# The first token group of a hybrid attention and mLSTM block: small inputs in one array, low weight parts on VectorE, a third stage tile

## The chip, the cores and the metric

The kernel runs on one core of one Trainium2 chip. The metric is the time of one execution in device microseconds. The kernel before takes 1304.31 us, the median of three runs (1303.35 to 1304.36).

## What is computed

One layer of an encoder trunk. A conditioning vector c gives a shift, a scale and a gate; x is RMS-normalised, scaled and shifted; one wide projection feeds a neighbourhood-attention head group and a bidirectional mLSTM head group; an output projection, the gated residual and a final RMSNorm follow. The part that matters here is the beginning:

```python
c_act = jax.nn.silu(c)
mod = c_act @ w_ada + b_ada
shift, scale, gate = jnp.split(mod, 3, axis=-1)
h = rmsnorm(x, norm_w) * (1.0 + scale) + shift
proj = h @ w_in + b_in        # 2048 tokens, D = 1024, over 4600 columns
...
x = rmsnorm(x + gate * (mixed @ w_out), final_norm_w)
```

Everything is in float32. The two mixers lie far behind the change.

## The kernel before

The 2048 tokens are worked on in four groups of 512 (g = 0 to 3), D in eight steps of 128 (k = 0 to 7). h is kept transposed, with D on the partitions. A product in float32 is made of three faster ones: h is held as a high part `hhi` and a low part `hlo`, a weight block as `whi` and `wlo`, and each product adds hi x hi, hi x lo and lo x hi. The high part is a copy by ScalarE into the type that rounds, the low part a subtraction of raw and high; until now VectorE makes some of these low parts of the weights and GpSimd (POOL) the others.

The front is the method `start`. It is recorded in the order in which it is written (a manual schedule), so each engine's instructions stand as the code has them. Its parts, in order:

- Loads. ScalarE's queue loads the conditioning vector `cact`, a row of it `c_all`, the shift's and scale's bias `bada` and the norm weight `nw`; SyncE's queue (SP) loads x tile by tile, eighteen tiles `mod_*` of the modulation matrix, pieces of the first two weight blocks (`load_p`), and the sixteen gate columns `rg`. Each SP load takes one of eight semaphores in turn and so waits until the eighth load before it has landed.
- TensorE runs matmuls on constants, `dense`, five of them, then spreads c over the partitions (`c`), then four more.
- The sums of squares of x tiles 0 to 3 (ScalarE and VectorE in turn), their inverse roots, and the scaling of x.
- The modulation: for step 0, and for the shift of step 1, TensorE forms it with matmuls of one column (`column`). For all else VectorE does: `mod(n)` is one dot product of a loaded tile with `c_all`; even n gives the scale `gT`, odd n the shift `shT`, of step n // 2.
- The eight k steps of group 0. `turned(k)` transposes x on TensorE, `first_h(k)` makes `hhi` and `h` on ScalarE and returns the subtraction `low` for VectorE; `split_p` makes the weight parts; `products(k)` issues 24 matmuls into two blocks' banks, `firsts` and `seconds`. A third weight block (`raw_w(2, 2, ...)`) goes to a borrowed tile `w_extra`.
- The evictions of groups (`vo_group`): VectorE adds the bias and writes a stage tile `stvo`, ScalarE applies a sigmoid to half of it, and a store takes it to the scratch `d_ck`. Two stage tiles take turns (`stage_tile`). In group 0 three weight blocks are evicted: 0, 1 and the one in `w_extra`. GpSimd sets a column of each stage to one before it is used.
- h for groups 1 to 3 comes from a transposed copy of x (`load_t`) through `make_h` (VectorE, ScalarE, VectorE), which needs the roots of its group spread by TensorE (`rb`, line 286). `next_h` hands these out between the evictions: for group 1, it begins behind the third tile of the third weight block. `vo_first` then issues the products of the next group, k by k.
- From there on the schedule goes to the table fills `d_t`, the token blocks and all later phases.

Of the kernel before, what the change touches and what calls it, by code (L numbers as in the profile page):

```python
# [8 lines left out]
F32 = mybir.dt.float32  # L9
F32R = mybir.dt.float32r  # L10
AF = mybir.ActivationFunctionType
ALU = mybir.AluOpType
# [3 lines left out]
P = 128  # L16
D = 1024
# [41 lines left out]
class Kernel:  # L59
    def __init__(self, tc, x, x_p, x_t, cT, c_row, w_mod, w_gt, b_ada, norm_w, w_main, w_gate, b_col, b_row, b_gate, conv_w, conv_b,  # L60
                 rpb, ml_w, w_out, fnw, out):
        self.tc, self.nc = tc, tc.nc
        self.x, self.x_p, self.x_t, self.cT, self.c_row, self.w_mod, self.w_gt = x, x_p, x_t, cT, c_row, w_mod, w_gt
        self.b_ada, self.norm_w = b_ada, norm_w
        self.w_main, self.w_gate, self.b_col, self.b_row = w_main, w_gate, b_col, b_row
# [151 lines left out]
    def start(self, left):  # L217
# [4 lines left out]
        badd = ada.tile([P, 2 * KT], F32, name="bada")  # L222
        nw = ada.tile([P, KT], F32, name="nw")
        nwb = ada.tile([P, KT], F32, name="nwb")
        cb = ada.tile([P, D], F32, name="c_all")
        cact = ada.tile([P, KT], F32, name="cact")
# [101 lines left out]
        rg = xp.tile([P, KT, 16], F32, name="rg")  # L328
        nc.sync.dma_start(rg, self.w_gate)
# [13 lines left out]
        for n in range(9):  # L343
            if n == 5:
                for j, ps in enumerate(wide):
                    nc.tensor.matmul(ps, self.ones[0:1, :], cb[0:1, j * GT : (j + 1) * GT], start=True, stop=True)
            nc.tensor.matmul(dense[:, :240], self.ident, self.big, start=True, stop=True)
# [27 lines left out]
        for tt in (1, 3):  # L375
            scale_x(tt, rst, slice(2 * P, D), nc.vector)
# [45 lines left out]
        parts, ssqs = [], {}  # L422
# [6 lines left out]

        for k in range(KT):  # L430
# [41 lines left out]
        ssqs[1] = xp.tile([P, 4], F32, tag="ssq", bufs=2, name="ssq_1")  # L472
# [29 lines left out]
        for g in range(NG):  # L502
# [26 lines left out]
            else:  # L529
# [7 lines left out]
                self.vo_group(2, 2, 0, brow=brow, tops=tops)  # L537
# [11 lines left out]
    def gate_row(self, pool):  # L549
# [3 lines left out]
        nc.sync.dma_start(cact, self.cT)  # L553
# [108 lines left out]
    def vo_group(self, h, slot, g, first=None, brow=None, tops=()):  # L662
        nc = self.nc
        st = self.stage_tile(f"stvo_{h}_{g}")
# [1140 lines left out]
_INS = ['x', 'x_p', 'x_t', 'cT', 'c_row', 'w_mod', 'w_gt', 'b_ada', 'norm_w', 'w_main', 'w_gate', 'b_col', 'b_row', 'b_gate', 'conv_w', 'conv_b', 'rpb', 'ml_w', 'w_out', 'fnw']  # L1805
# [3 lines left out]
def layout(inputs):  # L1809
# [16 lines left out]
    def block(n):  # L1826
# [12 lines left out]
        "cT": a["c"][0].reshape(KT, P).T,  # L1839
# [3 lines left out]
        "b_ada": a["b_ada"][0][: 2 * D].reshape(2 * KT, P).T,  # L1843
        "norm_w": a["norm_w"][0].reshape(KT, P).T,
        "w_main": np.stack([block(n) for n in range(len(blocks))]),
        "w_gate": w3[:, :, GATES:],
# [34 lines left out]
```

## Time and profile before

| | |
|---|---|
| median of three runs | 1304.31 us |
| the profiled execution | 1305.46 us |
| its span, first to last instruction | 1303.7 us |
| mean granted TensorE clock | 0.989 |
| DVE, ACT, POOL busy | 61%, 41%, 20% of the span |
| HBM traffic | 204 GB/s over the span |

The page divides the span into 40 slices; the first three of the TensorE clock read 7, 9 and 8 tenths, the others 9 or more. Those three are the front. A busy TensorE in these pages isn't TensorE at its peak, as matmuls are pipelined; what is read here is when it is idle, and which instruction it waits for. Line numbers are those of the kernel before.

### The profile page before, as it was taken

To read this page: it belongs to the slowest core of one execution; us is meant where nothing else is said; L and a number is where in the kernel's file an instruction comes from. 1 tells how busy PE (TensorE), PEld (TensorE's weight loads), DVE (VectorE), ACT (ScalarE), POOL (GpSimd) and SP (SyncE) were. 2 spreads that over 40 slices of the span, in tenths; PEclk is the share of its full clock that TensorE was granted. 3 is DMA by queue.
4 is the path that set the end of the run, shared out by engine and by line. 5 is a ranking of instruction groups with operands and counts; after the bars stand their busy time and mean duration, and the time that the engine had idled before them with its cause. 6 is when DMAs were issued, how large, how long until landed. Compare 5 with 4: busy or idle time off the path is not lost.

```text
span 1303.7 us, 22944 instructions
## 1 busy us (share of the span) xinstructions
PE 1277.4 (98%) x8170; PEld 1103.3 (85%) x8170; DVE 794.7 (61%) x2384; ACT 532.3 (41%) x1172; POOL 258.6 (20%) x385
## 2 busy tenths in 40 slices
PE   9889999999999999999999999999999999999997
PEld 8889999999888887788888888888877878778776
DVE  5876353112567565166677877777657676767664
ACT  4444243543234222123333323333357555555551
POOL 1400002441000000102212002212224332332541
PEclk7989999999999999999999999999999999999999
DMA  9799955997678763745756767656688744655551
GB/s 365 260 293 295 254 195 136 253 234 193 189 179 197 173 153 97 202 122 161 198 164 201 246 195 220 211 176 169 201 252 276 225 156 154 201 179 171 169 167 66
DMA packets 217514, 259.08 MB, mean 199 GB/s; under 512 B 23867, under 2 KB 164027, under 8 KB 217400
## 3 DMA queue, kind: packets, MB, share of 16 engines
q1 hardware_dynamic: 142294, 186.48, 49.8%
q0 software_dynamic: 13616, 37.28, 9.1%
q10 hardware_dynamic: 61490, 33.85, 9.1%
q8 instruction: 65, 1.06, 0.3%
q14 instruction: 49, 0.40, 0.1%
HBM read 173.05 MB, written 92.72 MB: 204 GB/s over the span
## 4 chain that ended last, share of the span: by engine, by line
PE 77%; issue 5%; ACT 3%; DVE 3%; DMA 2%; POOL 1%; POOLq 0%; SPq 0%; ACTq 0%; DVEq 0%
PE pq L1046 24%; PE y L1611 7%; PE pc L605 4%; PE pc L606 4%; PE pc L604 4%; PE pvo L604 3%; PE pvo L606 3%; PE pvo L605 3%; PE pO L1568 3%; PE pT L1553 2%; PE pv L606 2%; PE pv L605 2%; PE pv L604 2%; PE pS L1522 2%; PE pi L1285 2%
## 5 line engine op out<-in xcount | busy, mean ns | idle before, releaser
L1046 PE MATMUL pq<-hhi,whi_a 128*128 128x512 f32 x512 | 208.3, 407 | 0.9 <-ACT u L951 0.9
L1046 PE MATMUL pq<-hlo,whi_a 128*128 128x512 f32 x512 | 208.3, 407 | 0.0
L1046 PE MATMUL pq<-hhi,wlo_a 128*128 128x512 f32 x512 | 207.1, 405 | 0.9 <-POOL wlo_a L1020 0.9
L1046 PEld LDWEIGHTS pq<-hhi,wlo_a 128*128 128x128 f32 x512 | 96.7, 189 | 17.6 <-POOL wlo_a L1020 1.3
L1046 PEld LDWEIGHTS pq<-hhi,whi_a 128*128 128x128 f32 x512 | 96.7, 189 | 17.4 <-ACT u L951 1.3
L1046 PEld LDWEIGHTS pq<-hlo,whi_a 128*128 128x128 f32 x512 | 96.8, 189 | 16.2 <-issue 0.6
L1020 POOL TENSOR_TENSOR wlo_a<-rawq,whi_a 128x1024 fp32r<-128x1024 f32 x19 | 45.5, 2395 | 295.8 <-ACT whi_a L1019 284.1
L1534 ACT ACTIVATE ring<-ring,mn 128x480 f32<-128x480 f32 (+5 forms) x128 | 76.0, 595 | 56.9 <-DVE mn L1533 56.6
L1555 ACT ACTIVATE ring<-pT 96x384 f32<-96x384 f32 (+3 forms) x128 | 65.6, 513 | 64.1 <-PE pT L1553 62.3
L1611 PE MATMUL y<-hhi,wlo_a 128*128 128x512 f32 (+1 forms) x272 | 89.7, 396 | 0.6 <-ACT y L1618 0.6
L1611 PE MATMUL y<-hhi,whi_a 128*128 128x512 f32 x256 | 88.6, 410 | 0.0
L1288 ACT ACTIVATE num<-px,gtile 128x129 f32<-128x129 f32 x120 | 38.3, 366 | 112.4 <-PE px L1283 83.7
L1460 POOL DMA_DIRECT2D v<-d_vna x158 | 79.0, 506 | 26.0 <-DMA v<-d_vna 6.3
L1307 POOL TENSOR_TENSOR hm<-hm,ck 128x128 f32<-128x128 f32 x64 | 27.5, 430 | 250.1 <-DVE hm L1306 213.8
L1553 PEld LDWEIGHTS pT<-ident,ring 128*128 128x128 f32 (+2 forms) x416 | 50.4, 136 | 26.9 <-ACT ring L1555 12.3
L1553 PE MATMUL pT<-ident,ring 128*128 128x128 f32 (+2 forms) x416 | 67.0, 274 | 3.9 <-ACT ring L1555 3.9
L1533 DVE CUSTOM_DVE_ANT_0 ring<-pS,tab 128x480 f32<-128x480 f32 (+5 forms) x128 | 62.4, 540 | 7.1 <-PE pS L1522 6.0
L604 PE MATMUL pvo<-whi_b,hhi 128*128 128x256 f32 x224 | 64.0, 286 | 0.5 <-DVE gates L678 0.5
L606 PE MATMUL pvo<-whi_b,hlo 128*128 128x256 f32 x224 | 63.2, 282 | 0.0
L605 PE MATMUL pvo<-wlo_b,hhi 128*128 128x256 f32 x224 | 63.2, 282 | 0.0
L893 ACT ACTIVATE dec<-dec,gtile 128x128 f32<-128x128 f32 x128 | 41.4, 391 | 46.9 <-POOL dec L886 36.6
L676 DVE TENSOR_TENSOR stvo<-pvo,brow 128x256 f32<-128x256 f32 x60 | 24.9, 420 | 58.3 <-PE pvo L606 43.4
(336 smaller groups left out, 3371.4 us busy)
## 6 DMA issues: line engine op xcount, KB each, us to landing
ck<-d_ck SPq DMA_DIRECT2D x64, 384.5 KB, 3.5
rawq<-in_w_main_dram SPq DMA_DIRECT2D x28, 512.0 KB, 4.5
raw<-in_w_main_dram SPq DMA_DIRECT2D x18, 512.0 KB, 5.8
kv<-d_ck SPq DMA_DIRECT2D x64, 128.5 KB, 3.2
dec<-d_mneg SPq DMA_DIRECT2D x32, 256.0 KB, 6.1
d_ck<-dec ACTq DMA_DIRECT2D x32, 256.0 KB, 6.6
d_ck<-stvo SPq DMA_DIRECT2D x15, 514.0 KB, 4.5
d_qna<-qst ACTq DMA_DIRECT2D x30, 256.0 KB, 4.5
```

Of the source, the lines that this page charges most:

```text
L604: nc.tensor.matmul(ps, lhi(k), rhi(k), start=(k == 0), stop=False)
L605: nc.tensor.matmul(ps, lhi(k), rlo(k), start=False, stop=False)
L606: self.mark = nc.tensor.matmul(ps, llo(k), rhi(k), start=False, stop=(k == KT - 1))
L893: nc.scalar.activation(t[:, o, :], t[:, o, :], AF.Exp, bias=self.cols["g"][:, d, h, c : c + 1])
L1020: (eng or nc.gpsimd).tensor_tensor(lo[:, :, cs], raw, hi[:, :, cs].bitcast(F32), ALU.subtract)
L1046: self.mark = nc.tensor.matmul(patch_ps(ps) if patch else ps, w, self.htok(h, g, k, patch), start=(k == 0 and n == 0), stop=(k == KT - 1 a ...
L1460: queue.dma_start(chunks[key][r * nkc : (r + 1) * nkc, :], rows[r])
L1533: nc.vector.tensor_tensor_reduce(pt[:, :nk], ps, tabs[ct][:, j * nk : (j + 1) * nk], 1.0, 3e38, ALU.add, ALU.min, mn)
L1534: nc.scalar.activation(pt[:, :nk], pt[:, :nk], AF.Exp, bias=mn, scale=-1.0, accum_out=sums[:, j : j + 1])
L1553: nc.tensor.transpose(ps[:cs, i, :], U[u][j][:, i * cs : (i + 1) * cs], self.ident)
L1555: nc.scalar.activation(t[:cs, :nch, :], ps[:cs, :nch, :], AF.Copy)
L1611: nc.tensor.matmul(y, m[:, k, :], w[k][:, cs], start=(k == 4 and n == 0), stop=(k == 3 and n == 2))
```

## The change

It has five parts.

1. The conditioning vector, the bias, the norm weight and the gate columns are laid out beside each other in one array `small`, 160 numbers to a partition. One load on ScalarE's queue replaces three there and one on SP.
2. TensorE runs 12 `dense` matmuls instead of 9: five before c is spread, as before, and seven behind it instead of four.
3. All low parts of weights in the front are made by VectorE: six pieces of blocks 0 and 1, and the two halves of `w_extra`, which move a little in the order (`high_w2`, `low_w2`). GpSimd has none left.
4. `mod(2)`, the scale of step 1, is summed ahead of the first low part of h; the rest of x's tiles 1 and 3 is scaled behind the second block's first low part. The four sums of squares for group 1 are all made by ScalarE; VectorE made two of them.
5. The third stage of group 0 has a tile of its own, `stvo_third`. The two old stage tiles go on taking turns without it.

The core of the diff:

```diff
-        nc.scalar.dma_start(cact, self.cT)
+        nc.scalar.dma_start(small, self.small)
         nc.scalar.dma_start(cb[0:1, :], self.c_row)
-        nc.scalar.dma_start(badd, self.b_ada)
-        nc.scalar.dma_start(nw, self.norm_w)
...
-        rg = xp.tile([P, KT, 16], F32, name="rg")
-        nc.sync.dma_start(rg, self.w_gate)
...
-        for n in range(9):
+        for n in range(12):
...
-        for tt in (1, 3):
-            scale_x(tt, rst, slice(2 * P, D), nc.vector)
+        mod(2)
...
+        def load_w2(half):
+            w2.append(self.raw.tile([P, 4, 256], F32, tag=f"raw{half}", name=f"raw_2_{half}"))
+            nc.sync.dma_start(w2[half], self.w_main[2, :, 4 * half : 4 * half + 4, :])
+
+        def high_w2(half):
+            nc.scalar.activation(self.wslot[2][0][:, 4 * half : 4 * half + 4, :], w2[half], AF.Copy)
+
+        def low_w2(half):
+            hi, lo = (part[:, 4 * half : 4 * half + 4, :] for part in self.wslot[2])
+            nc.vector.tensor_tensor(lo, w2[half], hi.bitcast(F32), ALU.subtract)
...
+                for tt in (1, 3):
+                    scale_x(tt, rst, slice(2 * P, D), nc.vector)
...
-            if k + 1 < KT:
+            if 0 < k < KT - 1:
                 mod(2 * k + 2)
...
-            if k:
+            if 0 < k < KT - 1:
                 low()
...
-                    split_p(b, (k + 1) // 2)(nc.gpsimd)
+                    split_p(b, (k + 1) // 2)()
             if k in (1, 4):
-                parts += self.raw_w(2, 2, (k // 4,))
+                load_w2(k // 4)
...
-            if k in (5, KT - 1):
-                parts[k // 6]()
+            if k in (KT - 3, KT - 2):
+                high_w2(k - KT + 3)
+            if k == KT - 2:
+                low_w2(0)
+            if k == KT - 1:
+                for tt in range(4, 8):
+                    square(tt, ssqs[1])
+                low()
+                low_w2(1)
...
-        for j in (0, 2):
-            dot(xt[4 + j], xt[4 + j], 1.0, 0.0, ssqs[1][:, j : j + 1])
-            square(5 + j, ssqs[1])
...
-                self.vo_group(2, 2, 0, brow=brow, tops=tops)
+                third = xp.tile([P, 1032], F32, name="stvo_third").rearrange("p (o c) -> p o c", o=4)
+                self.vo_group(2, 2, 0, brow=brow, tops=tops, stage=third)
...
-        st = self.stage_tile(f"stvo_{h}_{g}")
+        st = self.stage_tile(f"stvo_{h}_{g}") if stage is None else stage
```

How it moves the instructions, in the order of each engine. VectorE at the first low part, from the first subtraction for weight block 0 (`wlo_a`) on; ISA rows are dot products (`junkv`) and the reads of their sums. Before:

```order
L364 TENSOR_TENSOR wlo_a<-rg,whi_a 128x8x16
L276 TENSOR_SCALAR x_167<-x_167,rst_223 128x768
L276 TENSOR_SCALAR x_171<-x_171,rst_223 128x768
L390 TENSOR_TENSOR hlo_103<-h_0_280,hhi_102 128x512
L316 TENSOR_TENSOR wlo_b<-wr_0_178,whi_b 128x512
L260 ISA junkv_293,gT<-mod_hi,c_all,nwb,nw 128x1024
L260 ISA gT 128x1
L260 ISA junkv_339,gT<-mod_lo,c_all,nwb,nw 128x1024
```

and of the change:

```order
L359 TENSOR_TENSOR wlo_a<-small,whi_a 128x8x16
L259 ISA junkv_261,gT<-mod_hi,c_all,nwb,small 128x1024
L259 ISA gT 128x1
L384 TENSOR_TENSOR hlo_103<-h_0_278,hhi_102 128x512
L315 TENSOR_TENSOR wlo_b<-wr_0_172,whi_b 128x512
L275 TENSOR_SCALAR x_163<-x_163,rst_220 128x768
L275 TENSOR_SCALAR x_167<-x_167,rst_220 128x768
L259 ISA junkv_337,gT<-mod_lo,c_all,nwb,small 128x1024
```

The dot of step 1 has moved ahead of the first low part of h (`hlo`), and the scaling of x behind the second block's low part. VectorE at the end of group 0, before:

```order
L390 TENSOR_TENSOR hlo_103<-h_6_550,hhi_102 128x512
L260 ISA junkv_556,shT<-mod_lo,c_all,bada 128x1024
L260 ISA shT 128x1
L390 TENSOR_TENSOR hlo_103<-h_7_582,hhi_102 128x512
L260 ISA junkv_613,ssq_612<-xs_473 128x1024
L260 ISA ssq_612 128x1
L260 ISA junkv_617,ssq_612<-xs_473 128x1024
L260 ISA ssq_612 128x1
L676 TENSOR_TENSOR stvo_0_644<-pvo_0_276,brow_129 128x2x128
```

and of the change:

```order
L384 TENSOR_TENSOR hlo_103<-h_6_547,hhi_102 128x512
L259 ISA junkv_553,shT<-mod_lo,c_all,small 128x1024
L259 ISA shT 128x1
L427 TENSOR_TENSOR w_extra<-raw_0_348,w_extra 128x1024
L384 TENSOR_TENSOR hlo_103<-h_7_581,hhi_102 128x512
L427 TENSOR_TENSOR w_extra<-raw_1_469,w_extra 128x1024
L688 TENSOR_TENSOR stvo_0_641<-pvo_0_273,brow_129 128x2x128
```

The two dots on x (`xs`) are gone from here and the two halves of the third block's low part (`w_extra`) have come, one ahead of the last low part of h and one behind it. TensorE's order is the same in both but for the three `dense` matmuls, and SP's but for the gate columns' load.

More of the change, by code (lines that the diff above doesn't have):

```diff
@@ L221, in start @@
         xp = self.xpool
-        badd = ada.tile([P, 2 * KT], F32, name="bada")
-        nw = ada.tile([P, KT], F32, name="nw")
+        small = ada.tile([P, 20 * KT], F32, name="small")
+        cact, badd, nw = (small[:, a * KT : b * KT] for a, b in ((0, 1), (1, 3), (3, 4)))
+        rg = small[:, 4 * KT :].rearrange("p (k c) -> p k c", k=KT)
         nwb = ada.tile([P, KT], F32, name="nwb")
         cb = ada.tile([P, D], F32, name="c_all")
-        cact = ada.tile([P, KT], F32, name="cact")
         own = ada.tile([P, 3, D], F32, name="mod_own")
@@ L420, in products @@
                 nc.tensor.matmul(ps, h, w, start=opens, stop=(k == KT - 1 and n == 2), skip_group_check=b == 1)
-        parts, ssqs = [], {}
+        w2, ssqs = [], {}
+        def load_w2(half):
[6 more added lines that the diff above has]
+            nc.vector.tensor_tensor(lo, w2[half], hi.bitcast(F32), ALU.subtract)
         def sums_x(tiles):
@@ L428, in sums_x @@
                 yield square(tt, ssqs[g])
+        ssqs[1] = xp.tile([P, 4], F32, tag="ssq", bufs=2, name="ssq_1")
         for k in range(KT):
@@ L552, in gate_row @@
         cact = pool.tile([P, KT], F32, name="cact2")
-        nc.sync.dma_start(cact, self.cT)
+        nc.sync.dma_start(cact, self.small[:, :KT])
         nc.scalar.activation(cact, cact, AF.Silu)
@@ L660, in vo_first, with vo_group @@
             yield
-    def vo_group(self, h, slot, g, first=None, brow=None, tops=()):
+    def vo_group(self, h, slot, g, first=None, brow=None, tops=(), stage=None):
         nc = self.nc
-        st = self.stage_tile(f"stvo_{h}_{g}")
+        st = self.stage_tile(f"stvo_{h}_{g}") if stage is None else stage
         nc.gpsimd.memset(st[:, :, 128:129], 1.0)
@@ L1802, in body @@
     Kernel(tc, *args).run()
-_INS = ['x', 'x_p', 'x_t', 'cT', 'c_row', 'w_mod', 'w_gt', 'b_ada', 'norm_w', 'w_main', 'w_gate', 'b_col', 'b_row', 'b_gate', 'conv_w', 'conv_b', 'rpb', 'ml_w', 'w_out', 'fnw']
+_INS = ['x', 'x_p', 'x_t', 'small', 'c_row', 'w_mod', 'w_gt', 'w_main', 'b_col', 'b_row', 'b_gate', 'conv_w', 'conv_b', 'rpb', 'ml_w', 'w_out', 'fnw']
 _OUTS = [((16, 128, 1024), 'float32')]
@@ L1838, in layout @@
         "x_t": a["x"][0].T.reshape(KT, P, NG, GT).transpose(2, 1, 0, 3),
-        "cT": a["c"][0].reshape(KT, P).T,
+        "small": np.concatenate(
+            [a["c"][0].reshape(KT, P).T, a["b_ada"][0][: 2 * D].reshape(2 * KT, P).T, a["norm_w"][0].reshape(KT, P).T, w3[:, :, GATES:].reshape(P, 16 * KT)],
+            axis=1,
+        ),
         "c_row": a["c"],
```

11 lines of the change are left out of this document (3 added, 8 removed).

## Prediction

> **What bounds the kernel now.** I read the page first, then stretches of the span with the busy time of each engine, and then the front of the program instruction by instruction. In the first two rows below, the page's busy line says that TensorE (PE) is busy 98% of the span; the rows of the stretches give start:end, length, busy time and count of PE, its weight loads, VectorE (DVE), ScalarE and GpSimd, then the granted clock, the DMA share and GB/s.
>
> ```profile
> PE 1277.4 (98%) x8170; PEld 1103.3 (85%) x8170; DVE 794.7 (61%) x2384; ACT 532.3 (41%) x1172; POOL 258.6 (20%) x385
> 10.00:15.00 5.00, 4.95 (x30) 4.98 (x31) 4.54 (x21) 1.23 (x3) 0.00 (x0) 0.66 1.02 326
> 20.00:25.00 5.00, 5.00 (x25) 5.00 (x25) 3.34 (x6) 1.43 (x4) 0.00 (x0) 0.50 1.03 401
> 25.00:30.00 5.00, 5.00 (x30) 5.00 (x29) 4.01 (x4) 3.04 (x5) 3.51 (x2) 0.64 1.04 404
> 70.00:75.00 5.00, 3.78 (x15) 3.46 (x16) 4.73 (x8) 3.84 (x7) 0.10 (x1) 0.50 1.03 284
> 95.00:100.00 5.00, 5.00 (x43) 5.00 (x43) 4.07 (x8) 3.75 (x7) 0.00 (x0) 1.00 1.10 350
> ```
>
> From 95 us on PE is full at full clock: whatever time the front gives back there, the rest passes on, unless a load comes late. The front loses time in two ways: PE at half clock (0.50), and PE idle. The long idle stretches are these, in the PE timeline (start, length, what; in brackets the idle time before it and what ended it):
>
> ```profile
> 45.44 0.40 PE L420 MATMUL pvo<-whi_a,hhi 128*128 128x272 f32 x1 [0.54 <-ACT hhi L389]
> 49.53 0.77 PE L420 MATMUL pvo<-whi_a,hlo 128*128 128x272 f32 x4 [1.87 <-DVE hlo L390]
> 51.61 0.39 PE L420 MATMUL pvo<-whi_a,hhi 128*128 128x272 f32 x1 [0.84 <-ACT hhi L389]
> 71.17 0.59 PE L659 MATMUL pvo<-whi_a,hhi 128*128 128x272 f32 x1 [3.57 <-ACT hhi L397]
> ```
>
> The first three lie in the eight k steps of the first token group, where VectorE is late; the fourth lies behind the third weight group.
>
> **Low weights on VectorE, squares on ScalarE.** Three rows give VectorE's dots (L260), its low parts of h (L390) and GpSimd's work in the same stretch; then single instructions.
>
> ```profile
> 18.00:57.40 39.40, 26.40 (x30) 0.86 0.83 314
> 18.00:57.40 39.40, 8.28 (x8) 0.86 0.83 314
> 18.00:57.40 39.40, 17.01 (x10) 0.86 0.83 314
> 40.01 1.34 DVE L260 CUSTOM_DVE_ANT_0 junkv<-mod_hi,c_all,nwb 128x1024 bf16<-128x1024 f32 x1
> 45.59 3.34 POOL L209 TENSOR_TENSOR w_extra<-raw,w_extra 128x1024 fp32r<-128x1024 f32 x1
> 46.64 2.84 DVE L390 TENSOR_TENSOR hlo<-h,hhi 128x512 fp32r<-128x512 f32 x1
> 52.26 0.69 DVE L390 TENSOR_TENSOR hlo<-h,hhi 128x512 fp32r<-128x512 f32 x1 [1.58 <-ACT h L389]
> 13.11 0.68 DVE L316 TENSOR_TENSOR wlo_a<-raw,whi_a 128x512 fp32r<-128x512 f32 x1
> 143.67 1.22 DVE L209 TENSOR_TENSOR wlo_a<-raw,whi_a 128x1024 fp32r<-128x1024 f32 x1 [1.78 <-ACT whi_a L208]
> L256 ACT ACTIVATE junk<-xs 128x1024 bf16<-128x1024 f32 x2 | 2.1, 1056 | 0.0
> ```
>
> The same subtraction takes VectorE 0.69 us alone and 2.84 us beside GpSimd's 3.34 us: it finished half a microsecond after GpSimd did. Fifteen dots at about 1.36 us (with the read of the sum) would be 20.4 us, not 26.4; eight subtractions at 0.69 would be 5.5, not 8.28. So GpSimd's 17.0 us cost VectorE some 8.8 us. The change takes these eight GpSimd instructions away and gives VectorE six at 0.68 and two at 1.22, 6.5 us; two dots on x, 2.7 us, go to ScalarE as squares of 1.06 us. VectorE's work from the second dot of the chain on becomes 26.4 + 8.3 - 8.8 - 2.7 + 6.5, about 30 us. It can start at 14.0 (behind the row at 13.11 and the small gate part), or when the load of that dot is there, say 14.5: **VectorE's own floor is 44.5 us**, and the last products follow its last low part of h by 16 matmuls, so no end before about 46.3.
>
> The four squares on ScalarE stand where it is otherwise idle until the first eviction; they end some 5 us after the last h, beside the third weight group's matmuls, and the roots that need them are due only three tiles later. Cost nothing; without that cover 2.1 us, the two that are added.
>
> The dot of tile 1 ahead of the first low part costs nothing if its load is there. If not, the first low part waits for it with 8 matmuls behind, and all else on VectorE. From nothing to 1.5 us; I take 0.5, in the start above.
>
> **Small inputs in one array.** The gate weights come in 64-byte pieces. From 10 to 15 us the queues are full but move 326 GB/s instead of 401: (401-326)/401 x 5 = 0.9 us of DMA time. SP issues one load less, ScalarE two less. This makes loads up to 1 us earlier; on the path it is counted only in the 14.5 above. The bigger first load (80 KB for 4 KB, 0.2 us at that rate) could hold back the first square; it is behind x anyway.
>
> **Third stage tile.** Rows: the waits, three timeline rows, the weight group's matmuls with first and last start, VectorE's last low part of that group, and PE when it next runs dry.
>
> ```profile
> DVE stvo L676 <- DMA d_ck<-stvo: 5.2, 1, 5.2
> 63.67 1.05 PE L286 MATMUL rb<-diag,ones 128*128 128x128 f32 x8
> 68.62 1.09 DVE L676 TENSOR_TENSOR stvo<-pvo,brow_x 128x256 f32<-128x256 f32 x3 [5.17 <-DMA d_ck<-stvo]
> 69.62 1.40 DVE L396 SCALAR_TENSOR_TENSOR h<-xt,gT,rb 128x512 f32<-128x512 f32 x2
> 82.27 0.75 DVE L398 SCALAR_TENSOR_TENSOR hlo<-h,shT,hhi 128x512 fp32r<-128x512 f32 x1 [0.79 <-ACT hhi L397]
> L604 PE MATMUL pvo<-w_extra,hhi x32: 277/283/365, 55.0 to 67.1; 128*128 128x256 f32 x32
> 86.00:86.50 0.50, 0.06 (x1) 0.00 (x0) 0.50 (x3) 0.00 (x0) 0.00 (x0) 1.00 1.21 213
> ```
>
> The products end and the third weight group starts at 55.0. Its 96 matmuls take 12.4 less 1.05 for rb, 0.118 us each. VectorE's three evictions wait 5.17 us for the store of the first stage, and the next h stand behind them: the first h is 14.6 us after 55.0. With a tile of its own nothing holds the evictions but PE: three tiles, 8.5 us, and rb, 1.05, so 9.6 us: **5.0 us less**. Late next is VectorE itself: from the first h to the last low part it takes 13.4 us (69.62 to 83.0), and PE needs about 1 us more. Now PE ends at 86.0, 16.4 us after the first h, since it ran at half clock after its idle time; 14.4 is what the supply allows: **2.0 us less**.
>
> **The clock and three more dense matmuls.** Rows of half a microsecond where the clock changes, and four of the PE timeline.
>
> ```profile
> 11.50:12.00 0.50, 0.50 (x5) 0.50 (x5) 0.41 (x3) 0.04 (x1) 0.00 (x0) 0.58 0.98 283
> 28.50:29.00 0.50, 0.50 (x6) 0.50 (x5) 0.10 (x3) 0.39 (x1) 0.50 (x1) 0.85 1.07 401
> 69.50:70.00 0.50, 0.00 (x0) 0.00 (x0) 0.50 (x2) 0.00 (x0) 0.00 (x0) 0.60 0.34 72
> 76.00:76.50 0.50, 0.50 (x5) 0.50 (x4) 0.50 (x2) 0.50 (x3) 0.00 (x0) 0.57 1.04 426
> 7.25 1.89 PE L347 MATMUL dense<-big,ident 128*128 128x240 f32 x8
> 10.05 5.56 PE L368 MATMUL mod<-cact,mod_hi 128*128 128x1 f32 x32 [0.91 <-DMA mod_hi<-in_w_mod_dram]
> 20.38 3.40 PE L368 MATMUL mod<-cact,mod_hi 128*128 128x1 f32 x16
> 26.35 1.06 PE L382 MATMUL tp<-ident,x 128*128 128x128 f32 x4
> ```
>
> The clock falls at 11.6, rises at 28.7, falls at 69.6, rises at 76.4: 17.1, 40.9 and 6.8 us apart, which are 5, 12 and 2 steps of 3.41. So it is decided at 8.2, 11.6, 15.0, 18.5, 21.9, 25.3. The step up to 11.6 held 0.9 us of dense matmuls (they end at 9.14) and one-column matmuls: fall. The step up to 69.6 held 1.4 us of matmuls: fall. The step up to 49.2 held 1.9: none. With seven dense matmuls behind c they end near 10.5, 2.3 us into the step: no fall at 11.6. The next step has one-column matmuls, transposes and hardly a product, so I take a **fall at 15.0**. Till then the 32 column records take half of 0.2125 us each (3.40 over 16), 3.4 us, and end near 13.9 instead of 15.6; x is scaled by 13.1, ahead of the row at 13.11. A group of transposes (half of 1.06) and one pass of ScalarE at half the width of a square (0.5 to 0.8) put the first product near 14.9. At half clock, then: weight block 0, twelve at 0.236, to 17.7, columns 3.4 to 21.1, block 1 another 2.8 to 23.9, transposes 1.06 to 25.0. The step up to 25.3 is full, so the clock rises there. Then the rest of k=1 with its transposes to 28.5, four steps of 3.4 (24 x 0.118 and half of 1.06) to 42.1, two of 2.85: 47.8, and 0.2 for small waits: **48.0 instead of 55.0**, 7.0 us less. The sum stands above VectorE's floor, so PE sets it.
>
> **Sum.** 7.0 + 5.0 + 2.0 = 14.0 us off the profiled execution (1305.46 us; its span is 1303.7). That is 1.15 above the median of 1304.31, so the median would be 1290.3; I say 1290.5.
>
> **Rivals.**
> 1. The clock falls at 11.6 all the same: the dense matmuls do not suffice. Then k=1 starts where it does now, 0.5 us later for the longer dense run, and only the idle times of this stretch go (0.5 + 1.9 + 0.8 and as much as 0.7 in small ones): 3.4 + 7.0 = 10.4, 1293.9. For it: one-column matmuls visibly count little. Chance 0.16.
> 2. The clock does not fall at 15.0, or only for one step. Then VectorE's floor of 46.3 decides: 8.7 + 7.0 = 15.7, 1288.6. For it: the transposes and the first products fill the end of the step. Chance 0.24. The Trainium skill, "TensorE: Matmul & The Clock Gate", in Part 1 (What's actually happening), says that half rate comes after at least one idle window of about 3.4 us and that the window runs free of the kernel's start. By the first, no such window is left and this rival holds; the trace speaks against it, since the clock fell at 11.6 with PE idle for only 0.91 us (the bracket at 10.05). By the second the steps above could lie elsewhere in another execution.
> 3. The loads become the bound. Three stretches, the same columns as above:
>
> ```profile
> 43.50:45.50 2.00, 1.46 (x13) 1.23 (x12) 1.96 (x3) 0.90 (x3) 2.00 (x1) 1.00 0.26 96
> 51.00:58.00 7.00, 6.27 (x49) 6.05 (x50) 5.71 (x8) 5.64 (x8) 3.18 (x3) 1.00 0.05 19
> 67.00:70.00 3.00, 0.60 (x6) 0.39 (x4) 1.38 (x4) 0.00 (x0) 0.11 (x1) 0.93 0.14 37
> 111.80 0.10 POOL L665 MEMSET stvo<- 128x4 f32 x1 [11.09 <-DMA d_ck<-stvo]
> 114.20 0.43 DVE L676 TENSOR_TENSOR stvo<-pvo,brow 128x256 f32<-128x256 f32 x1 [2.23 <-issue]
> ```
>
> The queues stand idle 1.5 + 6.7 + 2.6 = 10.7 us before 70, and are near full afterwards. If all loads had to come first, no more than these and the 0.9 could be gained; if half is lost to the order on SP, about 6: 1298. Against it: what is loaded behind 57 us is released by computation that moves forward too. Chance 0.12.
> 4. Slower: a stage store behind the table fills. The stage that VectorE writes at 114.20 was free at 111.80, 2.4 us earlier. If the queues move forward by over 2.4 us less than the computation, VectorE stands there as it did at 68, PE runs dry, the saved time comes back as this wait, and two clock steps at half rate (6.8 us) cost 3.4 on top: 1307.7. Chance 0.03.
> 5. The third tile frees nothing because another wait lies right behind, and VectorE's added work eats the rest: no change, 1304. Chance 0.03.
>
> **How the numbers follow.** Forecast 0.42, rivals 0.24, 0.16, 0.12, 0.03, 0.03. The likeliest is 1290.5. The range reaches from rival 2 with 1.1 us more (the loads' microsecond) to rival 3: 1287.5 to 1298.5. A measurement can tell about 0.2%, 2.6 us, from no change: the first four cases, 0.94, are faster by more, 0.03 the same, 0.03 slower.
>
> **What would show it.** The profile of the changed kernel should have no GpSimd subtraction before the first stage memset and no VectorE subtraction above 0.8 us; the third weight group starting near 48 us; the first h of group 1 some 9.6 us behind it, with no wait on a stage store; no half clock near 70. It is wrong in the clock if 15 to 25 us is full rate or 11.6 half; wrong in rivals 3 and 4's sense if PE waits over 2 us anywhere behind 60 us.

## The result

| | median of the runs, us | lowest to highest |
|---|---|---|
| before | 1304.34 (6 runs) | 1303.35 to 1308.78 |
| changed | 1295.17 (6 runs) | 1292.91 to 1298.76 |

The ratio is **0.9925, 95% interval 0.9908 to 0.9943**: the medians are 9.2 us apart, where 14.0 us were forecast. In a second sitting (the fifth experiment) the ratio was 0.9916 (0.9892 to 0.994), 10.4 us. The profiled execution took 1294.11 us with a span of 1292.3, 11.4 less than before. The changed kernel's own runs lie further apart than its distance from the forecast: of the twelve of both sittings, nine are from 1292.4 to 1295.2, three from 1297.3 to 1298.8. That needs an explanation too.

The busy line from the page of the changed kernel:

```profile
PE 1270.2 (98%) x8176; PEld 1095.9 (85%) x8176; DVE 789.2 (61%) x2388; ACT 533.8 (41%) x1176; POOL 241.9 (19%) x377
```

Stretches of it with the columns of the prediction (busy time and count of PE, weight loads, VectorE, ScalarE, GpSimd; granted clock, DMA share, GB/s):

```profile
10.00:15.00 5.00, 4.94 (x41) 4.56 (x40) 4.11 (x19) 1.70 (x6) 0.00 (x0) 1.00 0.96 346
15.00:20.00 5.00, 4.66 (x26) 4.42 (x27) 4.72 (x7) 3.62 (x5) 0.00 (x0) 0.66 1.03 409
20.00:25.00 5.00, 5.00 (x44) 5.00 (x44) 3.84 (x8) 4.08 (x7) 0.00 (x0) 1.00 1.03 402
70.00:75.00 5.00, 3.04 (x24) 2.80 (x23) 4.62 (x23) 0.00 (x0) 0.00 (x0) 1.00 1.22 152
15.28:45.38 30.10, 28.82 (x219) 27.62 (x217) 28.05 (x45) 19.43 (x29) 0.00 (x0) 0.94 1.03 403
```

The half clock from 11.6 to 28.6 has shrunk to one step (0.66 from 15 to 20, full rate from 20 on). From 70 to 75 the clock is full now, but PE is busy for 3.04 us of five. The last row runs from VectorE's first dot of the chain to the end of its last low part of h: PE and VectorE are both nearly full there.

The path behind it: the third weight group's matmuls in the view of their tile (min/median/max in ns, first and last start).

```profile
L616 PE MATMUL pvo<-w_extra,hhi x32: 278/283/365, 47.5 to 59.5; 128*128 128x256 f32 x32
```

Rows of VectorE's and PE's timeline around it, in order of time:

```profile
44.69 0.69 DVE L384 TENSOR_TENSOR hlo<-h,hhi 128x512 fp32r<-128x512 f32 x1 [0.44 <-ACT h L383]
...
57.19 1.40 DVE L390 SCALAR_TENSOR_TENSOR h<-xt,gT,rb 128x512 f32<-128x512 f32 x2 [0.47 <-PE rb L285]
71.92 0.29 PE L671 MATMUL pvo<-whi_a,hlo 128*128 128x272 f32 x1
72.72 0.88 DVE L280 TENSOR_SCALAR diag<-ident,rst 128x128 f32<-128x128 f32 x4
73.51 0.42 DVE L688 TENSOR_TENSOR stvo<-pvo,brow 128x256 f32<-128x256 f32 x1
74.17 0.36 PE L616 MATMUL pvo<-whi_b,hhi 128*128 128x256 f32 x1 [1.96 <-DVE gates L690]
```

The group starts at 47.5 (before 55.0), the first h follows 9.7 us behind (before 14.6) and waits for PE's `rb`, no longer for a store. The products of group 1 end at 72.2 (before 86.0): **13.8 us** earlier, almost exactly the 14.0 forecast. Then PE stands for 1.96 us, which it did for 0.5 before: the evictions of the finished banks stand on VectorE behind the roots and the diagonal for group 2, 3.0 us from 70.54 on. That gives back 1.4 us. Another microsecond goes behind 640 us. The largest wait of PE there that grew is the one for VectorE's `st` (2.3 us here, 1.2 before); but the second profile of the changed kernel, where it is 1.0, also loses 0.6 us behind group 2, and that of kernel 9 nothing, so this loss differs from one execution to the next and its cause stays open.

All profiles can be laid on each other by four places. Each row is one execution: those of kernels 3 and 8 took 8.5 and 2.0 us more than the medians of their runs, those of 1 and 7 took 2.4 and 1.9 less. Times in us:

| kernel | third weight group starts | first h, group 1 | first h, group 2 | span |
|---|---|---|---|---|
| before | 55.0 | 69.6 | 90.6 | 1303.7 |
| changed | 47.5 | 57.2 | 78.2 | 1292.3 |
| 1, nine dense matmuls | 48.4 | 58.1 | 79.1 | 1294.1 |
| 2, no third tile | 49.1 | 59.4 | 81.9 | 1295.7 |
| 3, GpSimd again | 62.5 | 72.2 | 94.7 | 1312.1 |
| 4, roots later | 47.2 | 57.0 | 75.9 | 1295.0 |
| 5, changed, again | 47.2 | 56.9 | 77.9 | 1291.8 |
| 6, tile used twice | 52.5 | 62.2 | 83.2 | 1295.1 |
| 7, both | 49.1 | 58.9 | 77.8 | 1291.7 |
| 8, before, tile alone | 57.5 | 67.2 | 89.7 | 1305.6 |
| 9, c later | 47.1 | 56.8 | 77.8 | 1291.2 |
| 10, all three | 49.2 | 58.9 | 77.8 | 1291.2 |
| 11, GpSimd, c later | 55.9 | 66.0 | 88.5 | 1301.9 |
| 12, before, VectorE | 50.0 | 63.6 | 84.6 | 1297.9 |

### The profile page after: what moved, and what is told of

It reads as the page before. It is cut to its first block, busy times and chain, and to the rows that moved or that the text cites. A ratio compares the mean times of both kernels' runs of the same rounds, so it can differ in the third digit from the quotient of the medians.

```text
span 1292.3 us, 22945 instructions
## 1 busy us (share of the span) xinstructions
PE 1270.2 (98%) x8176; PEld 1095.9 (85%) x8176; DVE 789.2 (61%) x2388; ACT 533.8 (41%) x1176; POOL 241.9 (19%) x377
## 4 chain that ended last, share of the span: by engine, by line
PE 73%; issue 8%; DMA 4%; DVE 3%; ACT 3%; POOL 2%; POOLq 0%; SPq 0%; ACTq 0%; DVEq 0%
PE pq L1058 22%; PE y L1623 5%; PE pc L617 4%; PE pc L618 4%; PE pc L616 4%; PE pvo L616 3%; PE pvo L618 3%; PE pvo L617 3%; PE pv L618 2%; PE pv L617 2%; PE pv L616 2%; PE pO L1580 2%; PE pT L1565 2%; PE pi L1297 2%; PE pS L1534 2%
## 5 line engine op out<-in xcount | busy, mean ns | idle before, releaser
L1546 ACT ACTIVATE ring<-ring,mn 128x480 f32<-128x480 f32 (+5 forms) x128 | 76.0, 595 | 57.0 <-DVE mn L1545 56.6
L1567 ACT ACTIVATE ring<-pT 96x384 f32<-96x384 f32 (+3 forms) x128 | 65.5, 512 | 64.1 <-PE pT L1565 63.6
L1565 PEld LDWEIGHTS pT<-ident,ring 128*128 128x128 f32 (+2 forms) x416 | 50.5, 136 | 26.1 <-ACT ring L1567 11.4
L1545 DVE CUSTOM_DVE_ANT_0 ring<-pS,tab 128x480 f32<-128x480 f32 (+5 forms) x128 | 62.4, 540 | 7.1 <-PE pS L1534 6.0
```

What stands on the lines that cost most here:

```text
L1545: nc.vector.tensor_tensor_reduce(pt[:, :nk], ps, tabs[ct][:, j * nk : (j + 1) * nk], 1.0, 3e38, ALU.add, ALU.min, mn)
L1546: nc.scalar.activation(pt[:, :nk], pt[:, :nk], AF.Exp, bias=mn, scale=-1.0, accum_out=sums[:, j : j + 1])
L1565: nc.tensor.transpose(ps[:cs, i, :], U[u][j][:, i * cs : (i + 1) * cs], self.ident)
L1567: nc.scalar.activation(t[:cs, :nch, :], ps[:cs, :nch, :], AF.Copy)
```

## The experiments

All ratios are to the kernel before, timed in the same sitting. Its median was 1306.38 us beside the first four, 1304.15 beside 5 to 8, 1304.88 beside 9 to 11 and 1305.5 beside 12.

### One part undone (1, 2, 3)

```diff
1:
-        for n in range(12):
+        for n in range(9):
2:
-                self.vo_group(2, 2, 0, brow=brow, tops=tops, stage=third)
+                self.vo_group(2, 2, 0, brow=brow, tops=tops)
3:
-                    split_p(b, (k + 1) // 2)()
+                    split_p(b, (k + 1) // 2)(nc.gpsimd)
...
-            nc.vector.tensor_tensor(lo, w2[half], hi.bitcast(F32), ALU.subtract)
+            nc.gpsimd.tensor_tensor(lo, w2[half], hi.bitcast(F32), ALU.subtract)
```

> The changed kernel with nine dense matmuls as before instead of twelve, all else as changed. Theory: the three extra ones keep the clock up through the step that ends at 11.6, where it fell before; without them the clock falls there and the third weight group starts near 51 instead of 47.5 us, so about 1298.5 us. Rival: the clock falls once at about 15.7 either way, or falls at neither, and the count of dense matmuls decides nothing: within 1 us of the changed kernel, 1294 to 1296.

> The changed kernel without the third stage tile. Theory: VectorE stands again about 5 us for the store of the first stage, PE runs dry for about 3.5 us before the second token group, and half clock follows; of the 7 us counted for the tile, about 2 are already lost in the changed kernel behind 72 us, so 5 us come back: 1300 us. Rival: the tile gives the full 7.0, since the half clock comes too: 1302 us. Second rival: all that goes in front of it makes the store land early enough, and the tile is worth under 1 us.

> The changed kernel with the low weights of blocks 0, 1 (from the second quarter) and 2 by GpSimd again, as before. Theory: GpSimd's 17 us stretch VectorE's own work by 8.8 us and take 6.5 us off it, so VectorE's floor moves from 46.3 to about 48.6, and the third weight group from 47.5 to about 48.6: 1296.5 us. Rival: PE's matmuls alone set the end of the products, no change: 1295. Second rival: single late low parts make PE wait as before (0.5 + 1.9 + 0.8 us): 1298.5 us.

Measured: 1298.25 us, 0.9937 (0.9922 to 0.9952); 1297.22, 0.9936 (0.9916 to 0.9957); 1305.46, **1.0001 (0.9982 to 1.002)**. The first two lose some 0.1% each against the changed kernel, inside the intervals, so the times don't show that either part is worth anything. In the first the clock did fall one step earlier, at 12.2, but rose at 19.0, and the group started at 48.4 instead of the 51 expected: the mechanism was there, and its size missed. That its median is close to the 1298.5 expected means little: the kernel before was 2 us slower in this sitting too. In the second, the second rival's "under 1 us" is nearest. The third alone loses everything the change brought, and much more than any of the three sentences expected.

That one part is worth 10 us and another next to nothing doesn't follow from the prediction's sum. Why the third tile is worth so little, in the second experiment: VectorE's wait for the store, and the first h.

```profile
58.41 1.09 DVE L687 TENSOR_TENSOR stvo<-pvo,brow_x 128x256 f32<-128x256 f32 x3 [4.28 <-DMA d_ck<-stvo]
59.42 1.40 DVE L390 SCALAR_TENSOR_TENSOR h<-xt,gT,rb 128x512 f32<-128x512 f32 x2
```

The wait is still there (4.28 us), but it ends 9.3 us behind the start of the group (49.1), not 13.6 behind as before. With the tile the first h comes 9.7 us behind the group, here 10.3: only 0.6 us of the 5 are left. (Group 2 starts 32.8 us behind it instead of 30.7; most of that is a half-clock step, from 77.7 to 81.1, behind the roots' wait.) The store now lands 5.4 us after its issue; before it took 8.7. The likely reason stands on the queue of SP. In the kernel before, VectorE's last dot on x and SP's four loads of x for group 2 (start, duration):

```profile
54.13 3.29 DVE L260 CUSTOM_DVE_ANT_0 junkv<-xs 128x1024 bf16<-128x1024 f32 x1
57.49 1.75 SPq L244 DMA_DIRECT2D xs<-in_x_dram  x4
```

The same loads in the second experiment:

```profile
44.78 2.91 SPq L243 DMA_DIRECT2D xs<-in_x_dram  x4
```

These loads go to a pool that takes the place of the front's pool, and VectorE's dots write their `junkv` there, so the loads are issued as the last dot has been read out: at 57.4 before, where the dots on x come last, and at 44.7 here, where the modulation's do, since the squares of ScalarE write elsewhere. About half of these 13 us come from all of VectorE being earlier: before, the modulation's last dot was done at 50.7. What counts is how the loads lie to the store. Before, the store was issued at 59.75, the last of the four loads landed at 66.95 and the store at 68.5; here these are 52.9, 56.5 and 58.3. The store lands 1.5 to 1.8 us behind the last load both times, and 3.6 us of the loads lie behind its issue instead of 7.2. Kernel 12 below, with the dots, agrees: last dot done at 50.67, loads at 50.73, store issued at 53.0, last load landed at 61.0 and the store at 62.4. No run undoes the squares alone.

### Roots behind the first eviction (4)

```diff
+        runs = {}
+
+        def late_roots(tiles, g):
+            spreads[g], runs[g] = spread(tiles, roots(tiles, ssqs[g]))
+            yield
...
                     if k == 4 and tiles:
                         self.token_tiles(g + 1)
-                        spreads[g + 1], run = spread(tiles, roots(tiles, ssqs[g + 1]))
+                        ready = late_roots(tiles, g + 1) if g == 1 else None
+                        if g > 1:
+                            spreads[g + 1], run = spread(tiles, roots(tiles, ssqs[g + 1]))
...
+                if g == 1:
+                    self.chain = ready
                 self.vo_group(0, 0, g, self.firsts)
+                if g == 1:
+                    run = runs[2]
```

> The changed kernel with one move behind it: the square roots and the diagonal for token group 2 (3.0 us of VectorE) stand behind the first eviction of group 1 instead of ahead of it. Theory: the wait of 1.96 us of PE at 74.2 us is caused by these 3 us alone; it goes, and with it 1.5 to 2.0 us: 1293.4 us. Rival: the diagonal is late now and PE waits for it ahead of rb, or the next eviction is late: no change, 1295.

Measured: 1296.23 us, 0.9926 (0.9914 to 0.9939), no gain. PE's 1.96 us are gone, and h of group 2 starts at 75.9, 2.3 us earlier than in the changed kernel, so the theory of the wait holds; the gain is then lost in a place that neither sentence named. In the changed kernel GpSimd prepares a stage tile as the store before it lands, and VectorE evicts into it:

```profile
101.12 0.10 POOL L677 MEMSET stvo<- 128x4 f32 x1 [10.69 <-DMA d_ck<-stvo]
101.79 0.42 DVE L688 TENSOR_TENSOR stvo<-pvo,brow 128x256 f32<-128x256 f32 x1 [2.24 <-PE pvo L618]
```

In kernel 4, the same eviction and what PE waits for behind it:

```profile
103.77 0.43 DVE L700 TENSOR_TENSOR stvo<-pvo,brow 128x256 f32<-128x256 f32 x1 [6.51 <-DMA d_ck<-stvo]
110.65 0.40 PE L683 MATMUL pvo<-whi_a,hhi 128*128 128x272 f32 x1 [1.31 <-DVE stvo L700]
113.18 0.39 PE L683 MATMUL pvo<-whi_a,hhi 128*128 128x272 f32 x1 [2.01 <-DVE stvo L700]
```

In the changed kernel the stage was ready 0.67 us before VectorE used it; before the change it had 2.4. Here the computation came earlier and the store, which stands on the queues behind the table fills, 2.7 us later: VectorE stood 6.5 us and PE ran dry for 3.3, after which the clock fell for a step, at 113.7. That is the prediction's fourth rival, met with 2 us more speed.

### The changed kernel again, the tile used twice, both edits, and the tile alone (5 to 8)

```diff
6, and with the edit of 4 in 7:
-                self.vo_group(1, 1, g)
+                self.vo_group(1, 1, g, stage=third if g == 2 else None)
8, in the kernel before:
+                third = xp.tile([P, 1032], F32, name="stvo_third").rearrange("p (o c) -> p o c", o=4)
-                self.vo_group(2, 2, 0, brow=brow, tops=tops)
+                self.vo_group(2, 2, 0, brow=brow, tops=tops, stage=third)
...
-        st = self.stage_tile(f"stvo_{h}_{g}")
+        st = self.stage_tile(f"stvo_{h}_{g}") if stage is None else stage
```

> The changed kernel itself once more, for a second trace and its spread. Theory: the step of the clock lies elsewhere in another execution, and the time follows it and the landing of the stage store that the third tile of group 2 waits for, near 101 us: median near 1295 us, runs from 1293 to 1299. Rival: the spread came from that one sitting; all runs lie within 1.5 us.

> The changed kernel with the third stage tile used a second time, for the second weight group of token group 2, whose evictions else wait for a store behind the table fills. Theory: that store, with 0.7 us to spare in the profile of the changed kernel and 3.3 us late in another, makes the spread; with it gone, 1293 us and runs within 2 us. Rival: the clock's step makes the spread: median within 1 us of the changed kernel, spread as large.

> The changed kernel with both: the roots behind the first eviction of group 1, and the third stage tile used again in group 2. Theory: the 2 us of the first edit were given back as the wait for that store (3.3 us of PE at 110 and 113); with the store out of the way both count, 1291.3 us. Rival: the loads behind it are the bound now and take the 2 us in another place, no gain over the changed kernel: 1295.

> The kernel before with the third stage tile alone. Theory of the prediction: 5.0 us for VectorE's wait and 2.0 for the half clock, so 0.9946 of the time before, 1297.3 us. Rival: the store comes late only because all of the front is late (without the tile the changed kernel lost about 1 us); but here the front is as late as before, so this rival says also 5 to 7 us. Second rival: the chain of the next h, or the wait for a stage store behind the table fills, takes it back: under 3 us.

Measured: 1293.74 us, 0.9916; 1294.38, 0.9922 (0.9899 to 0.9944), spread 4.8 us; 1295.29, 0.9922 (0.9901 to 0.9943); 1305.43, 0.9993 (0.9975 to 1.001).

The spread stays with the tile used twice, so the store doesn't make it. Kernel 7 shows no gain in its median, as its rival said, while its trace kept it as far as group 2 (49.1 at the third group, 77.8 at group 2: 28.7 us, where the changed kernel takes 30.7), with no wait of PE for a stage; where its runs lose it stays open. Kernel 8 shows the tile doing what was forecast at its place, 9.7 us from the group to the first h instead of 14.6, and then the roots' wait behind it (2.0 us of PE) with a half-clock step (85.6 to 89.0) that take much of it: so the second rival in its size, though by another wait than the two that it names (the stage store costs PE 0.7 us here). This trace stands for one kind of execution only. The twelve runs of kernel 8 fall into two groups, five from 1299.46 to 1303.01 us and seven from 1305.29 to 1307.47, and the profiled one, whose clock rose late, is in the upper; of the seventeen runs of the kernel before in this sitting five are from 1307.87 to 1309.38 and the others at most 1305.58. So "no gain" is true of the median, and the tile alone may be worth some us in the other group; no trace shows that.

The traces of 6 and 8 (and of 3) were late from the start, though their recorded clock reads 1.00 up to 17 and 85 us. The first rows of PE in the changed kernel (the spread of c; dense matmuls, two records each; one-column matmuls):

```profile
5.72 1.98 PE L341 MATMUL c<-c_all,ones 1*128 1x512 f32 x4
7.63 3.10 PE L342 MATMUL dense<-big,ident 128*128 128x240 f32 x14
10.57 3.68 PE L363 MATMUL mod<-small,mod_hi 128*128 128x1 f32 x32
```

In kernel 6:

```profile
5.87 3.78 PE L341 MATMUL c<-c_all,ones 1*128 1x512 f32 x4
9.57 5.26 PE L342 MATMUL dense<-big,ident 128*128 128x240 f32 x14
14.66 4.34 PE L363 MATMUL mod<-small,mod_hi 128*128 128x1 f32 x32
```

In kernel 8:

```profile
5.86 3.78 PE L346 MATMUL c<-c_all,ones 1*128 1x512 f32 x4
9.57 3.57 PE L347 MATMUL dense<-big,ident 128*128 128x240 f32 x8
12.93 6.83 PE L368 MATMUL mod<-cact,mod_hi 128*128 128x1 f32 x32
24.37 1.84 PE L368 MATMUL mod<-cact,mod_hi 128*128 128x1 f32 x16
```

The same four matmuls for c take 1.98 us or 3.78. PE starts at half rate in all these traces; the clock record begins only where full rate does, at 5.5 us in the changed kernel's profile, at 14.0 in 6, at 24.1 in 8 (there the one-column matmuls go from 0.213 us each to 0.115). Kernel 6 reached the third weight group 5.3 us later than kernel 5, which has the same front. This is what the prediction didn't know of.

### The clock's first rise (9, 10, 11)

```diff
9, 10 and 11:
-            if n == 5:
+            if n == 8:
                 for j, ps in enumerate(wide):
10: also the edits of 4 and 6
11: also the edit of 3
```

> The changed kernel with the two products for c behind eight of the twelve dense matmuls instead of five. Theory: PE starts at half rate in every execution and goes to full rate at the first step of 3.41 us that holds some 2.85 us of dense matmuls; with five of them, 4.3 us at half rate, that fails for some phases of the step (rise at 14 instead of 5 us), which costs 4 to 5 us in about every third run. Eight last up to 8.4 us and always hold such a step: no run above 1295.5, median 1293.5. Rival: the slow runs have another cause, the spread stays as it was (1292.4 to 1298.8).

> The same with the roots behind the first eviction of group 1 and the third stage tile used again in group 2. Theory: with the clock's rise out of the way these two count 2 us here, whatever the phase: median 1291.5. Rival: something behind takes it back (in the profile of the two alone the start of token group 2 was 2.8 us earlier by it, 0.5 of that were lost later): no gain, 1293.5.

> The same as the first of this set with the low weights of blocks 0, 1 and 2 by GpSimd again. Theory: without the slow start, what is left is VectorE's work stretched by 9.6 us less the 6.5 it is spared, 3 us, the idle times of PE that it makes at the end of the products (5.6 us in the profile with the slow start), and a half clock of two steps behind them, 3.4 us: 6 to 9 us, 1300 to 1302.5. Rival: the 10 us measured were the slow start alone: 1295 to 1296.

Measured: 1294.3 us, 0.9926 (0.9914 to 0.9938), runs from 1292.96 to 1295.92; **1292.25, 0.9906 (0.9891 to 0.9921)**, runs from 1290.92 to 1292.99; 1304.11, 0.9998 (0.9985 to 1.001).

With eight dense matmuls ahead of c no run of 9 or 10 is above 1296 (one passed the bound of 1295.5 by 0.4), and full rate came by 7.1 us in all three profiles. That this took the late runs away is likely and not shown: they were three in twelve, and nine runs without one are then a chance of about one in 13; kernel 7, with five dense matmuls ahead of c, had none above 1296.4 in six; and two of kernel 11's twelve runs still lie 4 us above its median. The median of 9 isn't better than the changed kernel's. Kernel 10 has the lowest median of all, 2.05 us below 9 as expected, but on four runs and five, with overlapping intervals and profiles of the same span (1291.2 us). Its VectorE rows show the roots in their new place: eviction, diagonal, and PE's `rb`, with no wait of PE.

```profile
72.88 0.43 DVE L700 TENSOR_TENSOR stvo<-pvo,brow 128x256 f32<-128x256 f32 x1 [0.54 <-PE pvo L683]
75.47 0.88 DVE L280 TENSOR_SCALAR diag<-ident,rst 128x128 f32<-128x128 f32 x4
76.61 1.05 PE L285 MATMUL rb<-diag,ones 128*128 128x128 f32 x8
```

Kernel 11 settles that GpSimd's 10 us are not a matter of the start: its clock rose at 5.4 and fell from 15.6 to 19.1, that of 9 rose at 5.2 and fell from 15.5 to 18.9, and GpSimd's first subtraction comes at 22.9. The changed kernel's last dots and the low part between them, in VectorE's timeline:

```profile
37.54 1.28 DVE L259 CUSTOM_DVE_ANT_0 junkv<-mod_hi,c_all,small 128x1024 bf16<-128x1024 f32 x1
39.95 1.34 DVE L259 CUSTOM_DVE_ANT_0 junkv<-mod_hi,c_all,nwb 128x1024 bf16<-128x1024 f32 x1
41.22 0.69 DVE L384 TENSOR_TENSOR hlo<-h,hhi 128x512 fp32r<-128x512 f32 x1
41.82 1.28 DVE L259 CUSTOM_DVE_ANT_0 junkv<-mod_lo,c_all,small 128x1024 bf16<-128x1024 f32 x1
```

The same four in kernel 11 with the GpSimd row beside them, and the last low part:

```profile
38.94 2.34 DVE L259 CUSTOM_DVE_ANT_0 junkv<-mod_hi,c_all,small 128x1024 bf16<-128x1024 f32 x1
41.32 2.16 DVE L259 CUSTOM_DVE_ANT_0 junkv<-mod_hi,c_all,nwb 128x1024 bf16<-128x1024 f32 x1
42.35 6.12 POOL L427 TENSOR_TENSOR w_extra<-raw,w_extra 128x1024 fp32r<-128x1024 f32 x2
43.41 2.84 DVE L384 TENSOR_TENSOR hlo<-h,hhi 128x512 fp32r<-128x512 f32 x1
46.17 3.38 DVE L259 CUSTOM_DVE_ANT_0 junkv<-mod_lo,c_all,small 128x1024 bf16<-128x1024 f32 x1
51.14 0.69 DVE L384 TENSOR_TENSOR hlo<-h,hhi 128x512 fp32r<-128x512 f32 x1 [1.57 <-ACT h L383]
```

PE's waits between 40 and 60 us in kernel 11 (total, times, longest):

```profile
PE pvo L414 <- ACT hhi L383: 3.0, 2, 2.1
PE pvo L414 <- DVE hlo L384: 1.9, 1, 1.9
```

And two stretches of it, in the columns used above:

```profile
45.00:50.00 5.00, 2.11 (x8) 1.81 (x8) 4.57 (x3) 0.34 (x1) 3.59 (x5) 0.64 0.71 283
50.00:55.00 5.00, 4.51 (x20) 4.51 (x21) 2.55 (x10) 4.91 (x9) 0.00 (x0) 0.50 0.83 301
```

Four instructions that take VectorE 4.6 us alone take 10.7 here. They are the last links of the chain dot, h (ScalarE), low part (VectorE), so their 6.1 us pass straight to its end: 51.83 instead of 45.38 (45.00 in 9). The spared subtractions don't make up for it: where they stood VectorE now waits for ScalarE (1.57 us instead of 0.44). PE stands 4.9 us, the clock falls for 10.2 us (46.4 to 56.6), and h of group 1 starts 9.1 us later than in 9.

### VectorE's low weights alone (12)

```diff
in the kernel before:
-                    split_p(b, (k + 1) // 2)(nc.gpsimd)
+                    split_p(b, (k + 1) // 2)()
...
-                parts[k // 6]()
+                parts[k // 6](nc.vector)
```

> The kernel before with its eight GpSimd subtractions (low weights of blocks 0 and 1 from the second quarter, of block 2) on VectorE, and nothing else. Theory of parts that need each other: this one alone takes most of VectorE's late end away (51.8 instead of 45.4 us in the changed kernel with GpSimd); the front's late start and the store wait behind it stay: 0.9955 to 0.997 of the time before, about 1300 us. Rival: it alone is nearly all of the gain, since all the rest without it gave 0.9998: 0.993, 1296. Second rival, the sum of the prediction: VectorE's work from 18 us on becomes 26.4 + 8.3 - 8.8 + 6.5, its end 50.5, the products' 52.3 instead of 55.0: 2.7 us, 0.998.

Measured: 1300.11 us, 0.9965 (0.9949 to 0.998): 4.5 us by the ratio, 5.4 between the medians. That is the first theory; one rival lies outside the interval, the other at its edge. The third weight group in the view of its tile:

```profile
L604 PE MATMUL pvo<-w_extra,hhi x32: 278/283/365, 50.0 to 62.0; 128*128 128x256 f32 x32
```

And in the timeline PE's `rb`, which stands behind three tiles, GpSimd's first stage memset and the evictions:

```profile
58.63 1.05 PE L286 MATMUL rb<-diag,ones 128*128 128x128 f32 x8
62.52 0.10 POOL L665 MEMSET stvo<- 128x4 f32 x1 [60.92 <-DMA d_ck<-stvo]
62.60 1.09 DVE L676 TENSOR_TENSOR stvo<-pvo,brow_x 128x256 f32<-128x256 f32 x3 [5.92 <-PE pvo L606]
```

The group starts 5.0 us earlier (50.0), and then the three evictions still come 12.6 us behind it, all at once, although PE was through with three tiles at 58.6. The row puts the wait down to PE; GpSimd's shows that the store came last, at 62.5. So this part is worth some 5 us without the others and 10 with them, and the rest is worth nothing without it (kernels 3 and 11).

The times show this, and the trace of 12 only in part. VectorE's second low part of h and GpSimd's first subtraction in the kernel before:

```profile
25.59 0.69 DVE L390 TENSOR_TENSOR hlo<-h,hhi 128x512 fp32r<-128x512 f32 x1 [2.17 <-ACT h L389]
26.16 1.27 POOL L316 TENSOR_TENSOR wlo_a<-raw,whi_a 128x512 fp32r<-128x512 f32 x1 [24.65 <-ACT whi_a L315]
```

The same low part in kernel 12:

```profile
22.90 0.69 DVE L390 TENSOR_TENSOR hlo<-h,hhi 128x512 fp32r<-128x512 f32 x1
```

The clock fell at 11.6 and 11.8, but rose at 28.6 before and at 18.6 in 12. So 2.7 of the 5.0 us by which the group starts earlier were there before GpSimd would have begun, most of them by this execution's clock.

## Why the prediction was right, and where it was off

The direction, the three places and the order of size were right; that the first two terms agree so closely with the profile is in part luck, as the next paragraphs show.

**The three terms.** Measured on the same places as forecast: products of group 0 end 7.5 us earlier (7.0), first h 4.9 (5.0), end of group 1's products 1.4 (2.0). Together 13.8 of 14.0.

**The clock.** The fall came at 15.8 (forecast 15.0) and not at 11.6. The rise came after one step instead of three: that is the second rival's condition, and its bound, VectorE, decided. VectorE's floor of 46.3 assumed a start at 14.5; the start was 15.28, since the first dot waited for its load, which gives 47.1; measured 47.5. In kernels 2 and 7 the fall lasted three steps (16.2 to 26.5), as forecast, and the group started at 49.1. So forecast and second rival both occur, 1 to 2 us apart. The 7.0 came out at 7.5 because the two bounds lie that near to each other, and not because the steps were as forecast.

**VectorE and GpSimd.** No low part of 512 columns took more than 0.69 us in the front, as said, and the two of 1024 took 1.22 and 1.23, the price in the sum. The 8.8 us of contention were right in size: dots and low parts of h take 26.40 and 8.28 us before, 19.64 and 5.52 in kernel 12, 9.5 us less; kernel 11 against 9 gives 10.2. But the sum spread them over VectorE's whole work, as a floor, 8.8 less the 6.5 spared. 6.1 of them lie on the chain's last four links, and VectorE's end moved by 6.8 us from 9 to 11, not by 2.3; PE's idle time and the half clock behind it came on top. That is why the price of putting them back was 10 us and not 1 to 3.

**The third tile.** The 5.0 us were right against the trace of before, and not the tile's own, which is luck too. The squares on ScalarE, which the prediction put at "cost nothing", and VectorE's earlier end together moved SP's loads of x out of the store's way, and most of the same wait goes by that. With them, the tile adds 0.6 us at its place and about 1 us in the time, the latter within what the intervals can tell; alone (kernel 8) the median moved by 0.07%, within its interval.

**The step that failed** is "what is late next" behind group 1's products: PE's need of "about 1 us more" and then group 1's second weight group at once. There VectorE owed 3.0 us of roots ahead of the evictions. The trace of before had shown the end of that wait (0.5 us at 86.0): PE, slowed by the half clock, came late itself, and so hid the rest. It gave back 1.4 us. Removing it (4, 10) brought group 2 closer to the third weight group by 2 us.

**The rest of the gap,** from the 11.4 us of the profiles to some 10 of the medians, is where the runs differ. The changed kernel's two profiles had an early first rise and took 1294.11 and 1293.57 us, the one of kernel 6 a late one and 1296.88; single runs without a trace aren't shown to be of the one or the other kind, and kernel 9, whose rise came early by design, has no run above 1296, but only five runs. So the late rise as the cause of the gap is likely and not shown. That the sum was made against one profiled execution, which had an early rise, was a choice that the prediction named and did not price.

**Rivals 3 and 4.** The loads are not the bound up to 45 us: the queues are full from 15 on, but VectorE waits for a load once there, 0.5 us ahead of its first dot, and PE never. Of rival 4, 0.67 us were left before it set in, and kernel 4 met it.

## What to carry to other kernels

When several waits lie in a row, price each part also with the others already gone: here one part was worth some 5 us alone, 10 us with the rest, and the rest without it nothing. The contention of two engines cost most here where it lay on the last links of a chain, so ask where in time it lies and not only how much it is. And when a stage gets faster, look one eviction, one store and one buffer further: a wait of 0.5 us in the old trace was the visible end of one of 2 us.

## What the hardware showed that was not expected

- PE's first rise to full rate comes at a different time in each execution: 4.4 to 6.0 us in eight profiles with five dense matmuls ahead of c, but 14.0, 14.6 and 24.1 us in the other three. In all of them the later changes of the clock lie whole steps of 3.41 us behind the rise. Counted back by such steps, one with 2.9 us of dense matmuls sufficed (kernel 4, rise at 4.4, dense from 1.56 on), one with 2.8 did not (kernel 3, whose step ended at 4.3); that is two traces, and the bound may lie elsewhere. Matmuls with one row (c) or one column did not raise it: kernel 8 ran 10.6 us of them at half rate, and its step from 13.9 to 17.3 held one-column matmuls alone, without a rise. The clock row reads 1.00 for this time, so it has to be read from the durations.
- The Trainium skill, "TensorE: Matmul & The Clock Gate", in Part 1 (What's actually happening), says that the window runs free of the kernel's start. The profiles agree; the size of what follows from it, 5.3 us between two executions with one front, is seen here in kernels 5 and 6.
